# Scan matmuls of a hybrid HGRN2 and mLSTM block: full-array products in place of 64-row and 64-column ones

## The chip, the cores and the metric

One core of one Trainium2 chip runs one layer in one launch. The metric is device time in microseconds: the median of the runs of a kernel. All operands are float32.

## What is computed

One layer of a diffusion backbone for 128 prompt tokens and 256 sample tokens, width 2048: modulation (shift, scale and gate from silu(c) @ w_mod), a token mixer with an HGRN2 branch and an mLSTM branch, each scanned forward and backward with 8 heads, a merge, and a SwiGLU feed-forward net. The parts that the change touches, for one head and direction:

```
mod = silu(c) @ w_mod + b_mod                        # shift and scale of h
att = (q exp(b - b_ref)) (k exp(b_ref - b))^T        # HGRN2, causal, chunks of 64
qk  = (q k^T) exp(log_d - m_t)                       # mLSTM, m_t: row maximum
num = qk v + exp(g + m_0 - m_t) (q C_0)              # second term: the carried state
C   = sum_s exp(w_end - m) k_s v_s^T                 # new state of the prompt
```

mLSTM has 64 channels for q and k and 128 for v; HGRN2 has 128 for both.

## The kernel before

**The stream.** Every projection is W^T x with a 128x128 weight tile stationary and 384 tokens moving. Weights arrive in units of 1 MB (`load`, line 941, queue of SP), three on chip. Half a unit is a *piece*: 8 weight tiles. ScalarE rounds a piece to float32r (`wh`, line 356, called from `high`), VectorE makes the remainder (`wl`, line 953), and TensorE does three products a tile (lines 969 to 971), 24 a piece, 12,480 in all. Each accumulator is taken from PSUM by ScalarE or VectorE in `evac`.

**The work beside it.** The scans of both branches, the splits for the merge and the rest of the modulation are written as operations (`op(engine, cost, function, r=, w=)`), and `schedule` puts each in a slot before the products of a piece, in program order per engine, by its cost in us and its operands. `run_piece(i)` then issues: the load, `low(i + 1)`, the slot's operations, `high(i + 2)`, the products. So the costs written in the code set the order, not the time.

**Start.** For each of 16 column tiles j `mod1_half` makes rows of silu(c) @ w_mod in four column groups of the array, ScalarE copies them to `mvs`, and `mod1_end` (line 1099) sums the four groups: for shift and scale one product with `mvs` stationary and a 0/1 selector of two columns moving (line 1103). VectorE makes `shc` and `aac` of it (lines 1106, 1107), then `modulate` makes h's two parts.

**HGRN2, `hgrn(h)`.** GpSimd makes the cumulative sums (`cum`, lines 412 to 423). `fatt` (lines 479, 480) makes scores of 3 tiles of 128 tokens: the 128x128 product, then the block between the two chunks of the tile, 64x64, over part of it in PSUM. `fkt` transposes keys (line 487), `fds` makes state updates (line 498), `fo` the output (lines 517, 521).

**mLSTM rows, `rows()`.** The gates' cumulative sums run on GpSimd and the running maximum on VectorE, both through `scan` (lines 579 to 583), once per kernel, forward heads on partitions 0 to 7 and backward ones on 32 to 39. `fm` splits the row maxima M into `mh` and `ml`, 64 partitions each.

**mLSTM heads, `head(p, x, ...)`.** Two heads share a tile of q and of k, head x on partitions 64x to 64x + 63 (`rs`). `fqk` makes q k^T from 64 rows (lines 672 to 674). For each direction `fmb` spreads one row of M over 128 partitions with two products of 64 rows (lines 685, 686); VectorE adds the mask (`md`, line 690), ScalarE takes exponentials (`E`, `si`), VectorE multiplies (lines 708, 715, 716); `fnum` makes the numerator: intra products (line 727), and the carried term `si` times `c0`, 64 rows (line 730). `fcf` makes the new state, one product of 64 columns per direction (line 753); ScalarE copies it and GpSimd's queue writes it. Later the heads are normed and transposed (`fot`, line 786).

```
te.matmul(get(pa)[:, t], get(e2[d])[:, c], get(e1[d])[:, c], start=True, stop=True)
te.matmul(get(pa)[a0:a0 + 64, t, b0:b0 + 64], get(kl)[:, t], get(qb)[:, t], start=True, stop=True,
te.matmul(get(o)[:, l], get(si)[rs, (l - 1) * P:l * P], get(c0t)[rs, d], start=False, stop=True)
```

Of the kernel before, what the change touches and what calls it, by code (L numbers as in the profile page):

```python
# [37 lines left out]
# column starts in w_in  # L38
# [4 lines left out]
# columns of the packed vectors  # L43
# [8 lines left out]
V_SEL = 251  # L52
NVEC = 253

# columns of the constants
# [208 lines left out]
def body(ctx, tc, ws, wg, wm1, wm2, xt, vec, con, s0, c0, out_y, out_s, out_c, out_m, units, n_groups, late, trial):  # L264
    """late: the last piece beside which the scans run. trial: only plans, and returns where parts of it end."""
# [30 lines left out]
    # ================= the work beside the stream =================  # L296
    ops, tags, avail = [], {}, {}
    real, shapes = {}, {}
    for key, i in last_piece.items():
        if key[0] == "z":  # L300
            avail[key[1:]] = i
    Z = {}      # projected heads
    S = {}      # tiles that stay
    O = {}      # outputs of the heads

    caps = {"t": 7, "vn": 2, "s0": 2, "qb": 1, "kl": 1, "kp": 1, "kn": 1, "qx": 2, "dec": 2, "fin": 1, "s1": 2,
            "sc": 4, "o": 2, "c0": 2, "mkn": 2, "md": 1, "E": 2, "si": 2, "dn": 2, "hh": 2, "kw": 1, "cs": 1,
# [4 lines left out]
    for n in ("c0", "mkn", "md", "E", "si", "dn", "hh", "kw", "cs", "bst", "mv"):  # L312
        pool_of[n] = "mt"
# [52 lines left out]
    def hgrn(h):  # L366
# [34 lines left out]
        for d in range(2):  # L401
            w = lambda d=d: S["lw"][:, d, h:h + 1]  # noqa: E731
# [25 lines left out]
        for d in range(2):  # L428
            w = lambda d=d: S["lw"][:, d, h:h + 1]  # noqa: E731
# [46 lines left out]
            def fatt(d=d, pa=pa, kl=kl, qb=qb, a0=a0, b0=b0):  # L476
                for t in range(3):
                    c = slice(t * P, t * P + P)
                    te.matmul(get(pa)[:, t], get(e2[d])[:, c], get(e1[d])[:, c], start=True, stop=True)  # L479
                    te.matmul(get(pa)[a0:a0 + 64, t, b0:b0 + 64], get(kl)[:, t], get(qb)[:, t], start=True, stop=True,  # L480
                              skip_group_check=True)

            op("P", 1.0, fatt, r=[e1[d], e2[d], kl, qb], w=[pa])
# [62 lines left out]
    SEGS = ((0, NP), (NP, T))  # L546

    def rows():
# [46 lines left out]
        def fm():  # L595
# [3 lines left out]
            ve.tensor_copy(S["mh"], M)  # L599
            ve.tensor_tensor(S["ml"], M, S["mh"].bitcast(F32), ALU.subtract)  # L600
# [6 lines left out]
        op("D", 2.0, fm, r=["ra"], w=["rM", "rg", "we", "mh", "ml"])  # L607
# [43 lines left out]
    def head(p, x, mq, mk, c0t, kn, g):  # L651
# [26 lines left out]
        for d in range(2):  # L678
            i = 32 * d + h
            mb, md = N(f"mb{d}", "sc", (P, T)), N(f"md{d}", "md", (P, 3, P))  # L680
            e, si = N(f"e{d}", "E", (P, 4, P)), N(f"si{d}", "si", (P, 2 * P))

            def fmb(mb=mb, i=i):
                one = S["identr"][:, i:i + 1].to_broadcast([64, P])
                te.matmul(get(mb), one, S["mh"], start=True, stop=False)
                te.matmul(get(mb), one, S["ml"], start=False, stop=True)

            op("P", 0.33, fmb, r=["mh", "ml"], w=[mb], **g)
# [19 lines left out]
            op("D", cd(256), lambda si=si: ve.tensor_tensor(get(si)[rs], get(si)[rs], Z[mq][rs, NP:T], ALU.mult),  # L708
# [14 lines left out]
            def fnum(e=e, si=si, o=o, d=d, src=src):  # L723
                for l in range(3):
# [17 lines left out]
        kw, cf, cs = N("kw", "kw", (P, 2, 64)), N("cf", "sc", (64, 2, P + 1)), N("cs", "cs", (64, 2, P + 1))  # L742
# [141 lines left out]
    # ================= constants =================  # L884
# [10 lines left out]
    sel = vt[:, V_SEL:V_SEL + 2]  # L895
# [10 lines left out]
    # silu of the conditioning, padded to 32 columns  # L906
# [7 lines left out]
    # lower bound: softmax over the layer axis, first entry  # L914
# [19 lines left out]
    # ================= the weight stream =================  # L934
# [134 lines left out]
    # ================= start: modulation, h, the first heads =================  # L1069
# [14 lines left out]
    def mod1_half(j, half):  # L1084
        """Rows of silu(c) @ w_mod: four column tiles of the array at once, a quarter of k each."""
# [423 lines left out]
```

## Time and profile before

| | |
|---|---|
| median of 3 runs | 2459.87 us (2458.62 to 2460.76) |
| profiled execution, span from first to last instruction | 2456.4 us |
| TensorE busy | 2386.4 us, 14199 passes |
| VectorE, ScalarE, GpSimd busy | 1522.5, 929.1, 283.7 us |
| share of TensorE in the chain that ended last | 90% |

The profiled execution is known by its span alone; the runs' median is 3.4 us above it. In the profile a row of TensorE names the line, the tiles, then the array shape "rows\*columns", then the moving operand's partitions x elements. A float32 product is recorded as two passes, a float32r product or a transpose as one. Matmuls are pipelined: each lasts longer than the distance to the next, so distances between starts tell the rate. Times in rows are us from the span's start.

### The profile page before, as it was taken

To read this page: it belongs to the slowest core of one execution; us is meant where nothing else is said; L and a number is where in the kernel's file an instruction comes from. 1 tells how busy PE (TensorE), PEld (TensorE's weight loads), DVE (VectorE), ACT (ScalarE), POOL (GpSimd) and SP (SyncE) were. 2 spreads that over 40 slices of the span, in tenths; PEclk is the share of its full clock that TensorE was granted. 3 is DMA by queue.
4 is the path that set the end of the run, shared out by engine and by line. 5 is a ranking of instruction groups with operands and counts; after the bars stand their busy time and mean duration, and the time that the engine had idled before them with its cause. 6 is when DMAs were issued, how large, how long until landed. Compare 5 with 4: busy or idle time off the path is not lost.

```text
span 2456.4 us, 34520 instructions
## 1 busy us (share of the span) xinstructions
PE 2386.4 (97%) x14199; PEld 2313.9 (94%) x14199; DVE 1522.5 (62%) x2313; ACT 929.1 (38%) x1346; POOL 283.7 (12%) x332
## 2 busy tenths in 40 slices
PE   7999999999999999999996999999999999999995
PEld 5899889998999999999996999999999999999995
DVE  5777778776656888886758788334333433333337
ACT  5325555654445232223543333332233233223225
POOL 1115733320000000000415000000000000000002
PEclk9999999999999999999998999999999999999998
DMA  9863324333323666564432556333333333333331
GB/s 356 299 250 144 115 95 164 141 145 140 111 89 106 234 236 241 225 231 172 162 125 81 189 217 245 106 136 120 122 136 120 128 130 120 131 126 120 135 123 69
DMA packets 70541, 388.90 MB, mean 158 GB/s; under 512 B 8304, under 2 KB 10480, under 8 KB 37104
## 3 DMA queue, kind: packets, MB, share of 16 engines
q1 hardware_dynamic: 67824, 381.97, 42.3%
q0 software_dynamic: 1408, 3.16, 0.4%
q8 instruction: 111, 1.82, 0.3%
q10 hardware_dynamic: 1152, 1.57, 0.2%
q14 instruction: 46, 0.38, 0.0%
HBM read 381.95 MB, written 4.72 MB: 157 GB/s over the span
## 4 chain that ended last, share of the span: by engine, by line
PE 90%; DVE 5%; POOL 3%; ACT 1%; DMA 1%; issue 1%; SPq 0%; POOLq 0%; ACTq 0%; DVEq 0%
PE mm L969 28%; PE mm L971 28%; PE mm L970 28%; PE mv L1091 1%; DVE yacc L364 1%; PE o_o L727 1%; DVE wl L953 1%; POOL pp L579 1%; DVE modt L1059 1%; POOL cb L412 1%; PE o_o L730 1%; PE sc_pa L479 1%; DMA raw<-ws 1%; DVE lo L1064 0%; POOL pp L582 0%
## 5 line engine op out<-in xcount | busy, mean ns | idle before, releaser
L969 PE MATMUL mm<-hi,wh 128*128 128x384 f32 x3200 | 1088.9, 340 | 14.0 <-ACT hi L358 9.4
L971 PE MATMUL mm<-hi,wl 128*128 128x384 f32 x3200 | 1074.6, 336 | 8.4 <-DVE wl L953 8.4
L970 PE MATMUL mm<-lo,wh 128*128 128x384 f32 x3200 | 1073.7, 336 | 1.2 <-DVE lo L1064 1.2
L356 ACT ACTIVATE wh<-raw 128x1024 fp32r<-128x1024 f32 x520 | 548.5, 1055 | 557.2 <-PE mm L970 546.6
L953 DVE TENSOR_TENSOR wl<-raw,wh 128x1024 fp32r<-128x1024 f32 x520 | 635.9, 1234 | 64.7 <-ACT wh L356 64.4
L969 PEld LDWEIGHTS mm<-hi,wh 128*128 128x128 f32 x3200 | 604.2, 189 | 31.9 <-issue 14.0
L971 PEld LDWEIGHTS mm<-hi,wl 128*128 128x128 f32 x3200 | 603.8, 189 | 9.5 <-DVE wl L953 9.4
L970 PEld LDWEIGHTS mm<-lo,wh 128*128 128x128 f32 x3200 | 604.1, 189 | 3.2 <-DVE lo L1064 1.9
L815 DVE SCALAR_TENSOR_TENSOR acc_acc<-raw_w,st,acc_acc 128x512 f32<-128x512 f32 x480 | 335.1, 756 | 0.1
L969 PE MATMUL mm<-gh,wh 128*128 128x384 f32 x704 | 238.3, 338 | 0.0
L971 PE MATMUL mm<-gh,wl 128*128 128x384 f32 x704 | 238.0, 338 | 0.1
L970 PE MATMUL mm<-gl,wh 128*128 128x384 f32 x704 | 237.9, 338 | 0.0
L1048 DVE TENSOR_TENSOR yacc<-mm,yacc 128x384 f32<-128x384 f32 x80 | 44.6, 557 | 158.6 <-PE mm L971 158.6
L1033 DVE TENSOR_TENSOR fs<-mm,fs 128x384 f32<-128x384 f32 x44 | 24.6, 558 | 185.9 <-ACT fs L358 185.9
L364 POOL TENSOR_TENSOR yacc<-yacc,r 128x384 f32<-128x384 f32 (+1 forms) x6 | 7.5, 1247 | 1101.7 <-ACT r L358 1101.7
L971 PEld LDWEIGHTS mm<-gh,wl 128*128 128x128 f32 x704 | 132.2, 188 | 0.6 <-DVE wl L953 0.6
L969 PEld LDWEIGHTS mm<-gh,wh 128*128 128x128 f32 x704 | 132.2, 188 | 0.5 <-ACT yacc L356 0.4
L970 PEld LDWEIGHTS mm<-gl,wh 128*128 128x128 f32 x704 | 132.2, 188 | 0.4 <-DVE gl L844 0.4
L1038 DVE TENSOR_TENSOR fs<-mm,fs 128x384 f32<-128x384 f32 x44 | 24.5, 557 | 171.6 <-PE mm L971 171.6
L364 POOL TENSOR_TENSOR sum<-sum,part 128x384 f32<-128x384 f32 x29 | 34.5, 1189 | 510.5 <-ACT part L358 510.0
L970 PE MATMUL mm<-o,wh 128*128 128x384 f32 x256 | 86.3, 337 | 0.0
L969 PE MATMUL mm<-oh,wh 128*128 128x384 f32 x256 | 86.1, 337 | 0.0
(290 smaller groups left out, 1831.1 us busy)
## 6 DMA issues: line engine op xcount, KB each, us to landing
raw<-ws SPq DMA_DIRECT2D x260, 1024.0 KB, 4.9
raw_w<-wm SPq DMA_DIRECT2D x128, 512.0 KB, 3.4
wm<-wm SPq DMA_DIRECT2D x64, 512.0 KB, 6.4
xs<-xt SPq DMA_DIRECT2D x4, 768.0 KB, 7.0
x<-xt SPq DMA_DIRECT2D x4, 768.0 KB, 6.9
out_y<-yacc SPq DMA_DIRECT2D x8, 192.0 KB, 1.9
out_y<-yacc ACTq DMA_DIRECT2D x8, 192.0 KB, 1.9
s_s<-s POOLq DMA_DIRECT2D x8, 128.0 KB, 3.2
```

The source lines that it names most:

```text
L356: sc.activation(out, in_, func, bias=0.0, scale=scale)
L364: (gp if eng == "G" else ve).tensor_tensor(out, a, b, o)
L412: gp.tensor_tensor(y[:, :, 4:12], x[:, :, 4:12], x[:, :, 4 + sg * sh:12 + sg * sh], ALU.add)
L479: te.matmul(get(pa)[:, t], get(e2[d])[:, c], get(e1[d])[:, c], start=True, stop=True)
L579: en.tensor_tensor(Y[r, b + sh:e], X[r, b + sh:e], X[r, b:e - sh], o)
L815: ve.scalar_tensor_tensor(get(acc)[:, c], get(w)[:, i], col, get(acc)[:, c], ALU.mult, ALU.add)
L953: ve.tensor_tensor(lo, src, hi.bitcast(F32), ALU.subtract)
L969: te.matmul(acc, hi[:, s], xh, start=first, stop=False)
L970: te.matmul(acc, hi[:, s], xl, start=False, stop=False)
L971: te.matmul(acc, lo[:, s], xh, start=False, stop=last)
L1033: ve.tensor_tensor(s, acc, s, ALU.mult)
L1048: ve.tensor_tensor(yacc[j], acc, yacc[j], ALU.add)
```

## The change

- `fatt` issues its three 128x128 products first and its three 64x64 products after them; cost 1.0 to 0.8.
- `fm` writes M's two parts into one tile of 128 partitions, `mhl`; `identr` holds the identity twice, one below the other; `fmb` is one product of 128 rows; cost 0.33 to 0.17.
- `si` becomes four tiles that stay, 128 partitions high, whose half of the other head is set to zero once by GpSimd; `fnum` multiplies all 128 rows of `si` and `c0`; cost 1.3 to 1.2.
- `fcf` makes both directions in one product of 128 columns; the state's output has the order head, direction, key, value; cost 0.45 to 0.22, ScalarE's copy 258 to 129 columns.
- `mod1_end` transposes `mvs` (two transposes) and VectorE sums the four groups from PSUM (a reduction); the selector columns go; the constants, which hold the identity, are loaded before the first unit of the stream and not after it.
- Comments go, lines move by a few.

```diff
@@ plan of tiles
-            "sc": 4, "o": 2, "c0": 2, "mkn": 2, "md": 1, "E": 2, "si": 2, "dn": 2, "hh": 2, "kw": 1, "cs": 1,
+            "sc": 4, "o": 2, "c0": 2, "mkn": 2, "md": 1, "E": 2, "dn": 2, "hh": 2, "kw": 1, "cs": 1,
@@ fatt
                     te.matmul(get(pa)[:, t], get(e2[d])[:, c], get(e1[d])[:, c], start=True, stop=True)
+                for t in range(3):
                     te.matmul(get(pa)[a0:a0 + 64, t, b0:b0 + 64], get(kl)[:, t], get(qb)[:, t], start=True, stop=True,
                               skip_group_check=True)
-            op("P", 1.0, fatt, r=[e1[d], e2[d], kl, qb], w=[pa])
+            op("P", 0.8, fatt, r=[e1[d], e2[d], kl, qb], w=[pa])
@@ fm
-            ve.tensor_copy(S["mh"], M)
-            ve.tensor_tensor(S["ml"], M, S["mh"].bitcast(F32), ALU.subtract)
+            mh, ml = S["mhl"][0:64], S["mhl"][64:P]
+            ve.tensor_copy(mh, M)
+            ve.tensor_tensor(ml, M, mh.bitcast(F32), ALU.subtract)
@@ fmb
-                one = S["identr"][:, i:i + 1].to_broadcast([64, P])
-                te.matmul(get(mb), one, S["mh"], start=True, stop=False)
-                te.matmul(get(mb), one, S["ml"], start=False, stop=True)
-
-            op("P", 0.33, fmb, r=["mh", "ml"], w=[mb], **g)
+                te.matmul(get(mb), S["identr"][:, i:i + 1].to_broadcast([P, P]), S["mhl"], start=True, stop=True)
+
+            op("P", 0.17, fmb, r=["mhl"], w=[mb], **g)
@@ fnum
-                        te.matmul(get(o)[:, l], get(si)[rs, (l - 1) * P:l * P], get(c0t)[rs, d], start=False, stop=True)
+                        te.matmul(get(o)[:, l], S[si][:, (l - 1) * P:l * P], get(c0t)[:, d], start=False, stop=True)
-            op("P", 1.3, fnum, r=[e, si, va, c0t], w=[o], **g)
+            op("P", 1.2, fnum, r=[e, si, va, c0t], w=[o], **g)
@@ fcf
-            for d in range(2):
-                te.matmul(get(cf)[:, d], get(kw)[:, d], S[va][:, 0], start=True, stop=True)
-        op("P", 0.45, fcf, r=[kw, va], w=[cf], **g)
-        op("A", ca(258), lambda: act(get(cs), get(cf), AF.Copy), r=[cf], w=[cs], **g)
-        op("G", 1.1, lambda: gp.dma_start(out_c[h], get(cs)), r=[cs], **g)
+            te.matmul(get(cf), get(kw).rearrange("p d k -> p (d k)"), S[va][:, 0], start=True, stop=True)
+        op("P", 0.22, fcf, r=[kw, va], w=[cf], **g)
+        op("A", ca(P + 1), lambda: act(get(cs), get(cf), AF.Copy), r=[cf], w=[cs], **g)
+        op("G", 1.1, lambda: gp.dma_start(out_c[h].rearrange("d k v -> (d k) v"), get(cs)), r=[cs], **g)
@@ mod1_end
-        o = ps([P, 2, 2], "mvo", "sc", 3)
+        pt = ps([P, 2, P], "mvo", "sc", 3)
         for c in range(2):
-            te.matmul(o[:, c], sb[:, c * P:c * P + P], sel, start=True, stop=True)
+            te.transpose(pt[:, c], sb[:, c * P:c * P + P], S["ident"])
+        o = stp.tile([P, 2, 2], F32, tag="mvq", bufs=2, name="mvq")
+        ve.tensor_reduce(o, pt.rearrange("p s (q c) -> p s c q", c=32)[:, :, 0:2], mybir.AxisListType.X, ALU.add)
@@ start
     mod1_load(0)
+    sy.dma_start(ct, con)
     load(0)
-    sy.dma_start(ct, con)
@@ tiles
-    S["identr"] = mp.tile([64, 64], F32R, name="identr")
-    ve.tensor_copy(S["identr"], ct[0:64, 0:64])
+    S["identr"] = mp.tile([P, 64], F32R, name="identr")
+    for b in (0, 64):
+        ve.tensor_copy(S["identr"][b:b + 64], ct[b:b + 64, C_ID + b:C_ID + b + 64])
@@ mLSTM tiles
+        for d in range(2):
+            S[f"si{x}{d}"] = mtp.tile([P, 2 * P], F32, name=f"si{x}{d}")
+            gp.memset(S[f"si{x}{d}"][64 - 64 * x:P - 64 * x], 0.0)
```

How the order moves, in listings of the instructions as they are issued ("x2" is a row that repeats; sizes are those of the result, partitions x columns). First TensorE at the first `fatt` of the program, between the products of two pieces (sc_pa the scores, sc_pk the transposed keys). Before:

```order
L971 MATMUL mm<-hi,wl 128x384
L479 MATMUL sc_pa_2496<-t_e_2395,t_e_2389 128x128
L480 MATMUL sc_pa_2496<-qb_qb_2398,kl_kl_2444 64x64
L479 MATMUL sc_pa_2496<-t_e_2395,t_e_2389 128x128
L480 MATMUL sc_pa_2496<-qb_qb_2398,kl_kl_2444 64x64
L479 MATMUL sc_pa_2496<-t_e_2395,t_e_2389 128x128
L480 MATMUL sc_pa_2496<-qb_qb_2398,kl_kl_2444 64x64
L487 MATMUL sc_pk_2503<-ct,kp_kp_2446 128x128 x2
```

And with the change:

```order
L968 MATMUL mm<-hi,wl 128x384
L478 MATMUL sc_pa_2528<-t_e_2427,t_e_2421 128x128 x3
L480 MATMUL sc_pa_2528<-qb_qb_2430,kl_kl_2476 64x64 x3
L487 MATMUL sc_pk_2535<-ct,kp_kp_2478 128x128 x2
L966 MATMUL mm<-hi,wh 128x384
```

The six products are the same, in two runs of one shape.

Second, TensorE at the first numerators of mLSTM, at piece 100 (o_o the numerator, E_e the weights of the tokens, c_c the state c0, sc_pv the next head's values, sc_mb a row maximum). Before:

```order
L727 MATMUL o_o_5888<-va_5681,E_e_5788 128x129 x2
L730 MATMUL o_o_5888<-c_c_5688,si_si_5791 128x129
L727 MATMUL o_o_5888<-va_5681,E_e_5788 128x129 x2
L730 MATMUL o_o_5888<-c_c_5688,si_si_5791 128x129
L727 MATMUL o_o_5895<-va_5681,E_e_5796 128x129 x3
L730 MATMUL o_o_5895<-c_c_5688,si_si_5798 128x129
L727 MATMUL o_o_5895<-va_5681,E_e_5796 128x129
L730 MATMUL o_o_5895<-c_c_5688,si_si_5798 128x129
L664 MATMUL sc_pv<-ct,z_mv 128x128 x3
```

And with the change:

```order
L726 MATMUL o_o_5919<-va_5713,E_e_5827 128x129 x2
L729 MATMUL o_o_5919<-c_c_5728,si_5715 128x129
L726 MATMUL o_o_5919<-va_5713,E_e_5827 128x129 x2
L729 MATMUL o_o_5919<-c_c_5728,si_5715 128x129
L665 MATMUL sc_pv<-ct,z_mv 128x128 x3
L685 MATMUL sc_mb_5930<-mhl,identr 128x384
```

The backward numerator has moved to piece 101, and a row maximum of the next head, now one product, stands in its place.

Third, TensorE at the end of mLSTM with the change, pieces 126 and 127 (sc_ot the transposed output of the head before). Between the rows of line 685 and that of line 784 stand the 24 products of piece 126:

```order
L685 MATMUL sc_mb_7348<-mhl,identr 128x384
L685 MATMUL sc_mb_7356<-mhl,identr 128x384
...
L784 MATMUL sc_ot<-ct,hh_hh_7236 128x128 x3
L726 MATMUL o_o_7400<-va_5719,E_e_7352 128x129 x2
L729 MATMUL o_o_7400<-c_c_6630,si_5721 128x129
```

The numerator of the last head stands one piece behind its row maximum; before, no numerator stood closer than two pieces. The same distance of one piece stands at pieces 124 and 125.

## Rows read from the trace of the kernel before

**Rows 1.** The page's first line.
```profile
span 2456.4 us, 34520 instructions
```
**Rows 2.** Table by stretches: busy us (instructions) of each engine, granted clock, DMA share, GB/s.
```profile
208.00:292.00 84.00, 78.83 (x474) 75.66 (x474) 62.97 (x102) 48.09 (x78) 70.34 (x105) 1.00 0.37 143
326.00:762.00 436.00, 434.10 (x2570) 405.18 (x2570) 293.77 (x553) 224.49 (x400) 76.64 (x100) 1.00 0.34 123
292.50:295.90 3.40, 3.40 (x13) 3.40 (x12) 3.30 (x10) 3.37 (x7) 1.64 (x3) 0.50 0.21 58
```
**Rows 3.** TensorE's timeline: start, duration, instruction; the stream's products.
```profile
394.74 0.33 PE L969 MATMUL mm<-hi,wh 128*128 128x384 f32 x1
...
400.80 0.34 PE L971 MATMUL mm<-hi,wl 128*128 128x384 f32 x1
```
**Rows 4.** The same timeline: an output of HGRN2, all on the full array.
```profile
344.30 0.60 PE L517 MATMUL o_po<-t_as,vn_vn 128*128 128x128 f32 x4
...
346.03 0.34 PE L970 MATMUL mm<-lo,wh 128*128 128x384 f32 x1
```
**Rows 5.** The same timeline: one cycle of `fatt` and the start of the next.
```profile
410.93 0.49 PE L479 MATMUL sc_pa<-t_e,t_e 128*128 128x128 f32 x2 [1.32 <-DVE t_e L446]
411.34 0.33 PE L480 MATMUL sc_pa<-qb_qb,kl_kl 128*64 128x64 f32 x2
411.60 0.49 PE L479 MATMUL sc_pa<-t_e,t_e 128*128 128x128 f32 x2
```
**Rows 6.** The same timeline: transposes of 64 columns in the row work.
```profile
316.79 0.22 PE L621 MATMUL sc_rt<-ct,rg 64*128 64x64 f32 x1
...
317.10 0.22 PE L622 MATMUL sc_rt<-ct,we 64*128 64x64 f32 x1
```
**Rows 7.** Timeline of GpSimd, VectorE, TensorE near 290 us, idle time before and its releaser.
```profile
285.09 1.00 POOL L364 TENSOR_TENSOR ra<-ra,rg 64x384 f32<-64x384 f32 x1
286.13 1.49 DVE L579 TENSOR_TENSOR pp<-ra 32x127 f32<-32x127 f32 x1 [5.70 <-POOL ra L364]
291.40 0.49 PE L521 MATMUL o_po<-qx_qx,s_s 128*128 128x128 f32 x2 [3.54 <-DVE s_s L505]
```
**Rows 8.** TensorE's timeline: first pass of one head's numerators, and what follows them.
```profile
572.06 0.61 PE L727 MATMUL o_o<-va,E_e 128*128 128x129 f32 x4
...
576.19 0.55 PE L664 MATMUL sc_pv<-ct,z_mv 128*128 128x128 f32 x3
```
**Rows 9.** The same timeline: a row maximum beside q k of the other rows.
```profile
581.18 0.38 PE L673 MATMUL sc_qa<-z_mq,z_mk 64*128 64x256 f32 x1
581.18 0.44 PE L685 MATMUL sc_mb<-mh,identr 64*128 64x384 f32 x1
```
**Rows 10.** The same timeline: the products around a row maximum that stands alone.
```profile
557.10 0.34 PE L971 MATMUL mm<-hi,wl 128*128 128x384 f32 x1
...
558.19 0.34 PE L970 MATMUL mm<-lo,wh 128*128 128x384 f32 x1
```
**Rows 11.** The same timeline: the products around a new state that stands alone.
```profile
566.92 0.34 PE L971 MATMUL mm<-hi,wl 128*128 128x384 f32 x1
...
568.05 0.33 PE L970 MATMUL mm<-lo,wh 128*128 128x384 f32 x1
```
**Rows 12.** Timeline of TensorE and VectorE at `mod1_end` of j = 2.
```profile
44.42 0.50 PE L1103 MATMUL mvo<-vt,mvs 128*128 128x2 f32 x4
...
45.04 0.33 PE L970 MATMUL mm<-lo,wh 128*128 128x384 f32 x1
45.09 0.21 DVE L1106 TENSOR_SCALAR shc<-mvo,vt 128x2 f32<-128x2 f32 x1
```
**Rows 13.** Timeline: a row maximum and the last VectorE operation on its E.
```profile
721.10 0.42 PE L685 MATMUL sc_mb<-mh,identr 64*128 64x384 f32 x1
...
725.76 0.41 DVE L716 TENSOR_TENSOR E_e<-E_e,sc_qb 128x256 f32<-128x256 f32 x1
```
**Rows 14.** DMA issues of the first 60 us: KB each, median us to landing.
```profile
raw<-ws SPq DMA_DIRECT2D x5, 1024.0 KB, 12.4
```

More of the change, by code (lines that the diff above doesn't have):

```diff
@@ L51 @@
 V_C = 219
-V_SEL = 251
-NVEC = 253
+NVEC = 251
 C_ID, C_UP, C_LO, C_BUP, C_BLO = 0, 128, 256, 384, 512
@@ L311, in body @@
         pool_of[n] = "hg"
-    for n in ("c0", "mkn", "md", "E", "si", "dn", "hh", "kw", "cs", "bst", "mv"):
+    for n in ("c0", "mkn", "md", "E", "dn", "hh", "kw", "cs", "bst", "mv"):
         pool_of[n] = "mt"
@@ L605, in fm @@
             ve.tensor_scalar(we, a[:, 0:NP], S["mT"], None, ALU.subtract)
-        op("D", 2.0, fm, r=["ra"], w=["rM", "rg", "we", "mh", "ml"])
+        op("D", 2.0, fm, r=["ra"], w=["rM", "rg", "we", "mhl"])
         def fmo():
@@ L680, in head @@
             mb, md = N(f"mb{d}", "sc", (P, T)), N(f"md{d}", "md", (P, 3, P))
-            e, si = N(f"e{d}", "E", (P, 4, P)), N(f"si{d}", "si", (P, 2 * P))
+            e, si = N(f"e{d}", "E", (P, 4, P)), f"si{x}{d}"
             def fmb(mb=mb, i=i):
-                one = S["identr"][:, i:i + 1].to_broadcast([64, P])
-                te.matmul(get(mb), one, S["mh"], start=True, stop=False)
-                te.matmul(get(mb), one, S["ml"], start=False, stop=True)
-            op("P", 0.33, fmb, r=["mh", "ml"], w=[mb], **g)
+                te.matmul(get(mb), S["identr"][:, i:i + 1].to_broadcast([P, P]), S["mhl"], start=True, stop=True)
+            op("P", 0.17, fmb, r=["mhl"], w=[mb], **g)
             c = C_BLO if d else C_BUP
@@ L698, in foff @@
                 cc = V_M0B + 8 * d + h
-                act(get(si)[rs], get(mb)[rs, NP:T], AF.Exp, bias=S["vt"][rs, cc:cc + 1], scale=-1.0)
+                act(S[si][rs], get(mb)[rs, NP:T], AF.Exp, bias=S["vt"][rs, cc:cc + 1], scale=-1.0)
             op("A", ca(P) + ca(256), foff, r=[mb, "ac"], w=[e, si], table="E", **g)
@@ L707, in head @@
             op("A", 3 * ca(P), fdiag, r=[md, "ac"], w=[e], table="E", **g)
-            op("D", cd(256), lambda si=si: ve.tensor_tensor(get(si)[rs], get(si)[rs], Z[mq][rs, NP:T], ALU.mult),
+            op("D", cd(256), lambda si=si: ve.tensor_tensor(S[si][rs], S[si][rs], Z[mq][rs, NP:T], ALU.mult),
                r=[mq], w=[si], **g)
@@ L741, in head @@
             op("D", cd(T) + 0.2, fh, r=[o, dn, "ac"], w=[hh[d], dn], **g)
-        kw, cf, cs = N("kw", "kw", (P, 2, 64)), N("cf", "sc", (64, 2, P + 1)), N("cs", "cs", (64, 2, P + 1))
+        kw, cf, cs = N("kw", "kw", (P, 2, 64)), N("cf", "sc", (P, P + 1)), N("cs", "cs", (P, P + 1))
         def fkw():
@@ L894, in body @@
     S["ident"] = ct[:, C_ID:C_ID + P]
-    sel = vt[:, V_SEL:V_SEL + 2]
     for n, v in (("eps", EPS), ("one", 1.0), ("zero", 0.0)):
@@ L1180, in body @@
     mp = open_pool("mk")
-    S["identr"] = mp.tile([64, 64], F32R, name="identr")
-    ve.tensor_copy(S["identr"], ct[0:64, 0:64])
-    S["mh"] = mp.tile([64, T], F32R, name="mh")
-    S["ml"] = mp.tile([64, T], F32R, name="ml")
+    S["identr"] = mp.tile([P, 64], F32R, name="identr")
+    for b in (0, 64):
+        ve.tensor_copy(S["identr"][b:b + 64], ct[b:b + 64, C_ID + b:C_ID + b + 64])
+    S["mhl"] = mp.tile([P, T], F32R, name="mhl")
     S["ac"] = mp.tile([P, 3, 64], F32, name="ac")
@@ L1456, in layout @@
     c0 = np.ascontiguousarray(cn.reshape(2, 4, P, P + 1).transpose(1, 2, 0, 3))
-    for q in range(4):
-        for k in range(2):
-            v[32 * q + k, V_SEL + k] = 1
     return {"ws": ws, "wg": wg, "wm1": wm1, "wm2": wm2, "xt": xt, "vec": v, "con": constants(), "s0": s0, "c0": c0}
-OUTS = {"out_y": (P, KT, T), "out_s": (2, 8, P, P), "out_c": (8, 64, 2, P + 1), "out_m": (2, 8, 1)}
+OUTS = {"out_y": (P, KT, T), "out_s": (2, 8, P, P), "out_c": (8, 2, 64, P + 1), "out_m": (2, 8, 1)}
 def find_lead():
@@ L1503 @@
     s, cn, m = (np.asarray(got[k]) for k in ("out_s", "out_c", "out_m"))
-    c = cn[..., 0:P].transpose(2, 0, 1, 3)
-    n = cn[..., P].transpose(2, 0, 1)
+    c = cn[..., 0:P].transpose(1, 0, 2, 3)
+    n = cn[..., P].transpose(1, 0, 2)
     r = np.ascontiguousarray
```

## The prediction

> **What bounds the kernel now.** I read the page first: the span is 2456.4 us [rows 1]. The median of the runs, 2459.87 us, is 3.4 us above it; I take that 3.4 us as what lies around the span and work against the span. Then I read the table by stretches: from 326 to 762 us, where most of the edited work lies, TensorE is busy 434 of 436 us at full clock, VectorE 294, ScalarE 224, GpSimd 77 [rows 2]. So there a nanosecond of TensorE is a nanosecond of the kernel. From 208 to 292 us it is another picture: GpSimd is busy 70 of 84 us and TensorE has waits [rows 2].
>
> Since matmuls overlap, busy time tells little; I read the timeline of TensorE and take distances between starts. The stream's products start 6.06 us apart over 35 steps, 0.173 us each [rows 3]; a piece of 24 of them is 4.16 us. For the other work I take the distance from the last start before it, less what the products alone would need. A float32 product is two passes in the records ("x2" is one product), a transpose one. In the plain case, seven products of 128 columns on the full array (14 passes, lines 517 and 521 in turn, other operands each time) take 1.73 us to the second product after them; less one step of 0.173 that is **0.111 us a pass**, say 0.112 [rows 4].
>
> Against this price, a pass that follows one of another array shape (the "128\*128", "128\*64", "64\*128" of a row) is dear. In `fatt` the same pair of lines returns every 0.67 us [rows 5]: two passes of 128 columns (0.224) and two of 64. Seven small transposes of 64 columns show 0.31 us for five steps, 0.062 a pass [rows 6]. So 0.67 - 0.224 - 0.124 = **0.32 us is two changes of shape**.
>
> **The change part by part.**
>
> *`fatt`* (16 times: 8 heads, 2 directions). Three shape cycles become one. Two cycles at 0.67 turn into four passes of each kind, 4 x 0.112 + 4 x 0.062 = 0.70: it saves 1.34 - 0.70 = 0.64 us each time. If a 64-column pass without a change cost 0.13 (half of the 0.26 us from 411.34 to 411.60 [rows 5], which holds a change), it would be 1.34 - 0.97 = 0.37. I take 0.64, since the small pass has a row of its own. But four of the 16 lie in the stretch from 208 to 292 us, where the pace is not TensorE's. At 291.40 TensorE has stood 3.54 us for VectorE's s_s (line 505), which stands in VectorE's queue behind the row scans of line 579, which at 286.13 had waited for GpSimd's ra [rows 7]. GpSimd is the bound of that stretch, so these four only lengthen the wait: 12 x 0.64 = **7.7 us** (4.4 to 7.7; 10.3 if all sixteen counted).
>
> *`fnum`, the carried term* (16 times). Both directions of one head, 24 passes, take from 572.06 to 576.19, 4.13 us [rows 8]. The zero-padded si lets all 24 run on the full array: 24 x 0.112 = 2.69, so 1.44 a head, 11.5 for eight. What is lost: a 64-row pass can run beside one that uses the other 64 rows. In two heads, and no more, the last c0 product of before runs beside the next head's line 672, in the way that lines 673 and 685 start together at 581.18 [rows 9]. A c0 product with its two changes costs (4.13 - 16 x 0.112) / 4 = 0.58, so at most 2 x 0.58 = 1.2 goes: **10.3 us**. The memsets of si on GpSimd are free: it is busy 77 of 436 us there [rows 2]; uncovered they would delay only the load of c0, which is issued several pieces before its first use.
>
> *`fmb`, row maxima* (16 times). Two 64-row products become one of 128 rows, one step of 0.173. Alone, the two cost 558.19 - 557.10 - 2 x 0.173 = 0.74 [rows 10]. Six stand alone; six stand in company and share a change of shape, which I count at 0.35 to 0.74; four stand beside the q k products of the other 64 rows and cost nothing [rows 9]. So 12 x 0.65 = 7.8 goes, 16 x 0.173 = 2.8 comes, **5.0 us**.
>
> *`fcf`* (8 times). Four passes become two. Alone: 568.05 - 566.92 - 2 x 0.173 = 0.78 [rows 11], new 0.224, so 0.56. Five of the eight follow a pass that had another shape anyway and pay one change less; mean 0.45: **3.6 us**. The copy and the write of the state get no longer and nobody waits for them.
>
> *`mod1_end`* (16 times). Four passes take (45.04 - 44.42 - 0.173) / 4 = 0.112 each although they move two columns [rows 12]; two transposes take two such passes, which saves 0.22. VectorE gets one reduction more before shc. Its price has no row: at least 0.21 (shc, which reads PSUM [rows 12]), at most 0.41 (a 128x256 operation from PSUM, line 716 [rows 13]); with 16 numbers read I take 0.21. It hides except for the first three j, where VectorE still adds partial sums and TensorE waits for it; there the saving is lost and the reduction paid. 13 x 0.22 - 3 x 0.21 = **2.3 us** (1.6 to 2.9).
>
> The constants (320 KB) now load ahead of the first unit. In the crowded start a unit of 1024 KB lands 12.4 us after its issue [rows 14]; 320 KB in front of it cost at most that share, 3.9 us, and at least nothing. I take nothing: ScalarE comes to the first unit only after the first hi, which hangs on x, the shift and the scale; that chain is the cover.
>
> *New waits.* TensorE's order stays the same up to piece 79 of the stream; in the mLSTM part the planner packs the shorter TensorE work tighter. From a row-max product to the end of its E (line 716) the chain takes 721.10 to 726.17, 5.07 us [rows 13]; in two places (the last listing in front shows one) the numerator now stands one piece behind the row-max product, 4.16 + 0.2. That is 0.7 us twice; with 0.6, a guess, for the tighter rest I take **-2 us** (0 to -8 if chains wait in every head).
>
> Sum: 7.7 + 10.3 + 5.0 + 3.6 + 2.3 - 2 = **26.9 us**. The span becomes 2429.5 and the time **2433.0 us**.
>
> A rule speaks against this change. The Trainium skill, "TensorEngine Tiling (Array Packing)", section Overview, has operands of at most 64 rows run as independent tiles, up to twice as fast. Were every c0 pass of before shared in that way, giving it up would cost another 32 x 0.112 = 3.6 us, and the sum would be 23.3 us, 2436.6; the trace shows such pairs in six places only [rows 9], since elsewhere the neighbour uses all rows.
>
> **Rivals.**
> 1. *Waits take half of the mLSTM gain.* The shorter slots leave VectorE and ScalarE less cover, and each of eight heads has two chains of about 5 us. One more microsecond in ten of the sixteen: 2433 + 10 = 2443. For it: one-piece distances are new. Against it: VectorE is busy 294 of 436 us, and almost nothing waits there now [rows 2].
> 2. *More comes through.* No new waits, and the absorbed four count: 2433 - 2 - 2.6 = 2428; without the lost overlap 2427.
> 3. *The cost is not the shape.* If only removed passes count, fmb wins (24 - 16) x 0.173 = 1.4, fcf 8 x 0.224 = 1.8, mod1_end 2.3, and 1.2 of overlap and 2 of waits are lost: 2.3 us, 2457.6, no change. Against it: lines 517 and 521 change operands without any extra [rows 4].
> 4. *Slower, by the clock.* After the 3.54 us wait the granted clock is 0.50 from 292.5 to 295.9, the lower of its two levels [rows 2, 7]. If the waits for E grow so long that TensorE's clock falls each time, one occurrence costs its wait and 4.16 us more for a piece at half clock. With 0.7 us waits it decides from 28.9 / 4.9, six occurrences; eight, one a head, are 39 us against 28.9 won, 2470. Against it: from 208 to 292 us TensorE's waits are 84.0 - 78.8 = 5.2 us in all and the clock is 1.00 [rows 2]; only after the longest of them did it fall, so 0.7 us should do nothing.
>
> **How the numbers follow.** The forecast, 2428 to 2440, has 0.70. Rival 1 (2440 to 2450) has 0.17, rival 2 below 2428 0.07, rival 3 0.04, rival 4 0.02. A range of 2426 to 2446 takes in rival 2 and the greater part of rival 1 and leaves out less than 0.2. A measurement of this kernel can tell about 0.2%, 4.9 us: faster 0.94, same 0.04, slower 0.02.
>
> **What would show it.** Right: `fatt` at about 1.35 us from its first pass to the transposes behind it, against three cycles of 0.67 now; a head's numerators at 2.7 us; row-max products 0.17 apart from their neighbours; no 64\*128 passes except q k and the seven small transposes; the wait for s_s near 290 us longer by 2 to 3 us; GpSimd's chain from 208 to 292 as long as now. Wrong: passes still 0.2 apart in runs of one shape (rival 3); waits of TensorE for E, hh or si between 550 and 762 us of over 5 us in all (rival 1); stretches of clock 0.5 there (rival 4).

## The result and the profile after

The changed kernel takes 2431.9 us (median of 4 runs, 2431.28 to 2432.88) beside 2459.24 us for the kernel before on the same chip: a ratio of 0.9887, 95% interval 0.9873 to 0.9901. The forecast was 2433.0 us. A second set of its runs gave 2429.64 us (2428.59 to 2433.35), ratio 0.9881 (0.9866 to 0.9895). One execution of one kernel below, 8628 us for e8_fatt_cut, is left out of all figures: its other three lie between 2438.8 and 2439.2, and no profile explains it.

The page's first line, then the table by stretches of the changed kernel (columns as in [rows 2]):

```profile
span 2429.2 us, 34432 instructions
```
```profile
208.00:292.00 84.00, 77.79 (x471) 75.61 (x470) 63.93 (x104) 47.57 (x77) 70.83 (x105) 0.98 0.38 145
326.00:762.00 436.00, 432.74 (x2689) 421.68 (x2688) 316.59 (x585) 240.29 (x427) 76.04 (x104) 1.00 0.37 136
49.90:53.30 3.40, 3.40 (x26) 2.05 (x28) 2.33 (x6) 0.00 (x0) 0.00 (x0) 0.50 0.02 5
271.70:275.10 3.40, 3.40 (x13) 3.40 (x12) 3.00 (x6) 2.29 (x5) 3.24 (x7) 0.50 0.00 0
```

The span is 27.2 us shorter. From 326 to 762 us TensorE is as full as it was [rows 2], but 2689 passes fit where 2570 did: the window holds more of the program. The stretch from 208 to 292 us did not get emptier on GpSimd (70.83 us against 70.34). Two stretches at the lower clock level, at 50 and 272 us, are new, and one that the trace of before has at 326.6 to 330.0 us is gone.

Now the edited places, in TensorE's timeline (start, duration, instruction). One `fatt` that nothing waits for:

```profile
437.81 0.34 PE L968 MATMUL mm<-hi,wl 128*128 128x384 f32 x1
437.99 0.83 PE L478 MATMUL sc_pa<-t_e,t_e 128*128 128x128 f32 x6
438.75 0.56 PE L480 MATMUL sc_pa<-qb_qb,kl_kl 128*64 128x64 f32 x6
439.24 0.44 PE L487 MATMUL sc_pk<-ct,kp_kp 128*128 128x128 f32 x2
439.44 0.42 PE L966 MATMUL mm<-hi,wh 128*128 128x384 f32 x1
```

From its first pass to the transposes (line 487): 439.24 - 437.99 = 1.25 us; to the product behind them 1.45. The same block in the trace of before, three cycles as in [rows 5], takes 446.03 - 443.91 = 2.12:

```profile
443.91 0.38 PE L479 MATMUL sc_pa<-t_e,t_e 128*128 128x128 f32 x2
...
446.03 0.42 PE L969 MATMUL mm<-hi,wh 128*128 128x384 f32 x1
```

One head's numerators, against 4.13 us [rows 8]:

```profile
579.21 0.61 PE L726 MATMUL o_o<-va,E_e 128*128 128x129 f32 x4
579.66 0.39 PE L729 MATMUL o_o<-c_c,si 128*128 128x129 f32 x2
...
581.81 0.42 PE L966 MATMUL mm<-hi,wh 128*128 128x384 f32 x1
```

24 passes in 2.60 us, 0.108 each; line 729, the carried term, now stands in the middle of line 726 without a seam. A row maximum alone (before: [rows 10]) and a new state alone (before: [rows 11]):

```profile
547.88 0.34 PE L968 MATMUL mm<-hi,wl 128*128 128x384 f32 x1
548.05 0.34 PE L685 MATMUL sc_mb<-mhl,identr 128*128 128x384 f32 x1
548.23 0.34 PE L966 MATMUL mm<-hi,wh 128*128 128x384 f32 x1
...
556.61 0.34 PE L968 MATMUL mm<-hi,wl 128*128 128x384 f32 x1
556.78 0.38 PE L751 MATMUL sc_cf<-va,kw_kw 128*128 128x129 f32 x2
556.92 0.42 PE L966 MATMUL mm<-hi,wh 128*128 128x384 f32 x1
557.18 0.33 PE L967 MATMUL mm<-lo,wh 128*128 128x384 f32 x1
```

The row maximum is one step among the stream's, 0.18 us where 0.74 went; the state costs 557.18 - 556.61 - 2 x 0.173 = 0.22 where 0.78 went. `mod1_end` at j = 2, TensorE and VectorE (before: [rows 12]):

```profile
44.23 0.38 PE L1100 MATMUL mvo<-ct,mvs 128*128 128x128 f32 x2
...
44.62 0.33 PE L967 MATMUL mm<-lo,wh 128*128 128x384 f32 x1
44.91 0.17 DVE L1102 TENSOR_REDUCE mvq<-mvo 128x4 f32<-128x16 f32 x1
45.10 0.23 DVE L1105 TENSOR_SCALAR shc<-mvq,vt 128x2 f32<-128x2 f32 x1
```

Two passes at 0.11 in place of four, and a reduction of 0.17 us before shc. Last, four waits of TensorE in the changed kernel (idle time and its releaser in brackets):

```profile
270.36 0.71 PE L498 MATMUL sc_pd<-vn_vn,kn_kn 128*128 128x128 f32 x4 [2.06 <-ACT kn_kn L355]
290.91 0.49 PE L521 MATMUL o_po<-qx_qx,s_s 128*128 128x128 f32 x2 [3.10 <-DVE s_s L505]
500.77 0.44 PE L487 MATMUL sc_pk<-ct,kp_kp 128*128 128x128 f32 x2 [0.50 <-DVE kp_kp L468]
713.83 0.71 PE L726 MATMUL o_o<-va,E_e 128*128 128x129 f32 x4 [0.67 <-DVE E_e L714]
```

The first is about twice as long as before (1.14 us), the second shorter than the 3.54 of [rows 7], the last two are new.

**Where the time went, by stage.** The stream is the same 12,480 products in every kernel here, so it is a ruler. I take the starts of its products number 120, 773, 1183, 2304 and 3161 (59.8, 204.9, 299.8, 551.0 and 765.0 us in the trace of before), counted from the first product, and subtract before. Negative is faster, in us. After the last mark no kernel differs by more than 0.25. The labels are those of the experiments below.

| kernel | to 60 | 60-205 | 205-300 | 300-551 | 551-765 |
|---|---|---|---|---|---|
| changed | +1.73 | -2.48 | +0.45 | -8.72 | -18.21 |
| changed, again (e11_again) | -1.35 | -2.48 | +0.50 | -7.10 | -18.22 |
| e1_fatt | -1.17 | 0.00 | -0.14 | -7.92 | 0.00 |
| e2_fnum | -0.33 | 0.00 | -0.01 | -0.02 | -9.87 |
| e3_fmb | -1.24 | 0.00 | -0.12 | +3.10 | -4.91 |
| e4_fcf | -0.30 | 0.00 | +0.04 | +0.02 | -3.33 |
| e5_mod | -0.52 | -2.48 | +1.20 | +1.44 | 0.00 |
| e6_oldcosts | +1.47 | -2.48 | +0.07 | -6.89 | -19.53 |
| e7_before_cut | -0.78 | 0.00 | -7.34 | -0.15 | 0.00 |
| e8_fatt_cut | -1.28 | 0.00 | -10.03 | -8.09 | 0.00 |
| e9_sel3 | -1.38 | -2.48 | +1.26 | -7.29 | -18.22 |
| e10_pad | -1.14 | -2.48 | -1.51 | -4.76 | -22.70 |
| e12_scan | -0.99 | -2.48 | -3.45 | -14.61 | -20.64 |

The columns 60-205 and 551-765 repeat to 0.01 us where the code is the same. The others carry stretches of low clock that come and go (last section), some 1.6 us each; "to 60" spreads by 1.3 us even among the kernels whose code is that of before there.

### The profile page after: what moved, and what is told of

It reads as the page before. It is cut to its first block, busy times and chain, and to the rows that moved or that the text cites. A ratio compares the mean times of both kernels' runs of the same rounds, so it can differ in the third digit from the quotient of the medians.

```text
span 2429.2 us, 34432 instructions
## 1 busy us (share of the span) xinstructions
PE 2355.8 (97%) x14135; PEld 2300.5 (95%) x14135; DVE 1527.1 (63%) x2330; ACT 928.2 (38%) x1346; POOL 283.8 (12%) x336
## 4 chain that ended last, share of the span: by engine, by line
PE 88%; DVE 6%; POOL 3%; ACT 2%; issue 1%; POOLq 0%; ACTq 0%; DVEq 0%
PE mm L966 28%; PE mm L968 27%; PE mm L967 27%; PE mv L1088 1%; DVE wl L950 1%; DVE yacc L363 1%; POOL cb L411 1%; POOL pp L579 1%; PE o_o L726 1%; DVE modt L1056 1%; DVE lo L1061 0%; PE sc_pa L821 0%; POOL pp L582 0%; ACT sq L357 0%; POOL sb L420 0%
## 5 line engine op out<-in xcount | busy, mean ns | idle before, releaser
L363 POOL TENSOR_TENSOR sum<-sum,part 128x384 f32<-128x384 f32 x29 | 34.3, 1183 | 499.6 <-ACT part L357 499.1
L355 ACT ACTIVATE gh<-fs 128x384 fp32r<-128x384 f32 x44 | 23.0, 524 | 166.4 <-DVE fs L1035 166.4
```

The lines of the kernel that those rows point to most:

```text
L355: sc.activation(out, in_, func, bias=0.0, scale=scale)
L363: (gp if eng == "G" else ve).tensor_tensor(out, a, b, o)
```

## The experiments

My theory (S in the expectations) was that TensorE pays for each change of array shape, that the five gains add, and that GpSimd's chain before 300 us swallows four of the sixteen in `fatt`. The rivals: only passes that go away count (P); the new order of the planner makes or breaks the gain; something other than GpSimd swallows.

**Each part alone, on the kernel before, with the planner's costs left alone so that the order stays.**

```diff
 e1_fatt
                     te.matmul(get(pa)[:, t], get(e2[d])[:, c], get(e1[d])[:, c], start=True, stop=True)
+                for t in range(3):
                     te.matmul(get(pa)[a0:a0 + 64, t, b0:b0 + 64], get(kl)[:, t], get(qb)[:, t], start=True, stop=True,
 e2_fnum
-                        te.matmul(get(o)[:, l], get(si)[rs, (l - 1) * P:l * P], get(c0t)[rs, d], start=False, stop=True)
+                        te.matmul(get(o)[:, l], S[si][:, (l - 1) * P:l * P], get(c0t)[:, d], start=False, stop=True)
 e3_fmb
-                te.matmul(get(mb), one, S["mh"], start=True, stop=False)
-                te.matmul(get(mb), one, S["ml"], start=False, stop=True)
+                te.matmul(get(mb), S["identr"][:, i:i + 1].to_broadcast([P, P]), S["mhl"], start=True, stop=True)
 e4_fcf
-            for d in range(2):
-                te.matmul(get(cf)[:, d], get(kw)[:, d], S[va][:, 0], start=True, stop=True)
+            te.matmul(get(cf), get(kw).rearrange("p d k -> p (d k)"), S[va][:, 0], start=True, stop=True)
```

> The kernel before with fatt's two loops alone, its cost left at 1.0, so that nothing else moves. Theory S (the change of array shape costs, and the stretch from 208 to 292 us, paced by GpSimd, swallows four of the sixteen): 12 x 0.67 = 8.0 us faster, some 2451 us; up to 324 us in the trace only 0.5 us won, the rest between 324 and 550. Theory A (no absorption): 16 x 0.67 = 10.7, 2448.5. Theory P (only passes that are removed count): no change, 2459.

> The kernel before with the zero-padded si alone, cost left at 1.3. Theory S: 8 heads x 1.5 us less 1.2 for two lost pairs of c0 beside q k: 10.3 to 11 us faster, some 2448.5 us, a head's numerators 2.67 us. Theory P: as many passes as before and lost pairs, 1 us slower, 2460. Rival W (the shorter slots turn into waits for E): under 6 us faster, and waits before line 727 or its kin over 4 us in all.

> The kernel before with one 128-row row-maximum product alone, cost left at 0.33. Theory S: 5.0 us faster (six alone at 0.56, six in company at about 0.3, four beside q k nothing or slightly slower), 2454. Theory P: 1.4 us faster, 2458.

> The kernel before with both directions' new state in one product of 128 columns alone, costs left. Theory S: 3.6 us faster (0.56 where it stands alone, 0.4 elsewhere), 2455.6. Theory P: 8 x 0.224 = 1.8 us, 2457.4. Both are near what the measurement can tell, so the distances between products in the trace decide: 0.22 a state where it was 0.78.

Measured, beside 2459.89 us for the kernel before (21 runs): 2449.98 us (ratio 0.9963, 0.995 to 0.9975), 2450.14 (0.9962, 0.9949 to 0.9974), 2454.75 (0.998, 0.9971 to 0.9989) and 2455.6 (0.9985, 0.9977 to 0.9994). (The zeroed tiles, the stacked tile and the order of the state's output, which these edits need, are as in the change.) In the stages that hold the edits: -8.06, -9.87, -4.91 and -3.33 us. Theory P falls with the first: it removes no pass at all, keeps the rest of the order, and wins 8 us. The second also keeps its passes and wins 9.9, a little under the 10.3 to 11 expected, with 575.12 - 572.45 = 2.67 us for a head's numerators:

```profile
572.45 0.61 PE L727 MATMUL o_o<-va,E_e 128*128 128x129 f32 x4
...
575.12 0.49 PE L664 MATMUL sc_pv<-ct,z_mv 128*128 128x128 f32 x3
```

In the last the trace decides: a state alone costs 0.23 us.

One more rival has to be met. e1_fatt also moves each 64x64 product away from the 128x128 product whose block of PSUM it writes over, so it could have won by that and not by the shape. e2_fnum rules this out as the general cause: it leaves the order and the place in PSUM as they were, its carried term adds to the block that the pass before has just written, and at full shape that goes at 0.11 us a pass. The changes of shape, counted in the traces, give the same price from three edits: 28 fewer and 4.69 us in e1_fatt (products 1715 to 2304), 54 fewer and 9.87 us in e2_fnum, 16 fewer and 3.17 us in e10_pad (below, beside e6_oldcosts), that is 0.17 to 0.20 us a change.

Where did the four `fatt` before 300 us go? TensorE's waits in e1_fatt from 204 to 299 us (waiting tile <- engine and tile waited for: us in total, times, longest):

```profile
PE o_po L522 <- DVE s_s L506: 4.4, 2, 4.2
PE sc_pd L499 <- ACT kn_kn L356: 2.0, 1, 2.0
PE sc_pa L481 <- DVE kl_kl L466: 0.3, 1, 0.3
PE sc_ss L527 <- ACT t_sq L358: 0.3, 1, 0.3
PE sc_pk L488 <- DVE kp_kp L469: 0.2, 1, 0.2
```

And in the kernel before, from 205 to 300 us:

```profile
PE o_po L521 <- DVE s_s L505: 3.5, 1, 3.5
PE sc_pd L498 <- ACT kn_kn L356: 1.1, 1, 1.1
PE sc_pa L480 <- DVE kl_kl L466: 0.5, 1, 0.5
```

7.2 us in all, where before had 5.2: of the 2.7 us won there 2.1 came back as waiting, spread over most of them. Stage 205-300 gained 0.14; the 0.5 between has no wait in the trace.

**`mod1_end` alone, and the order alone.** e5_mod is the kernel before with the transposes, the reduction and the constants' earlier load; e6_oldcosts is the changed kernel with the costs of before, all five of them:

```diff
-            op("P", 0.8, fatt, r=[e1[d], e2[d], kl, qb], w=[pa])
+            op("P", 1.0, fatt, r=[e1[d], e2[d], kl, qb], w=[pa])
...
-            op("P", 1.2, fnum, r=[e, si, va, c0t], w=[o], **g)
+            op("P", 1.3, fnum, r=[e, si, va, c0t], w=[o], **g)
```

> The kernel before with mod1_end's transposes and reduction, and the constants loaded ahead of the first unit, and nothing else. As predicted: 13 x 0.22 - 3 x 0.21 = 2.3 us faster, 2457. Theory W (read from the trace of the whole change): the reduction lengthens the chain to hi in the first places, TensorE stands 0.4 us longer there twice, and a stretch of half clock follows at about 50 us that costs some 0.8 us: 0.5 to 1.0 us won at 200 us in the trace, 2458.5. If the constants' earlier load held up the first unit, the first product of the stream would start later than the 30 us of before.

> The kernel with the whole change, but the planner's costs as before (1.0, 0.33, 1.3, 0.45 for TensorE, 258 columns for ScalarE's copy), so that the order is that of before wherever tiles allow. Theory S (the products' shape makes the gain): within 2 us of the whole change, 2431 to 2434. Rival O (the order matters): 5 us or more away from 2431.9, slower if the tighter packing is part of the gain, faster if the one-piece distances cost.

e5_mod: 2457.82 us beside 2460.38 (ratio 0.9993, 0.9984 to 1.0002), by itself not to be told from no change; but between 60 and 205 us it wins 2.48, the same as every kernel with this edit. With the first 60 us (0.52, which is within the spread of that column) it is 3.0 ahead at 205 us, not 0.5 to 1.0: there is no low clock at 50 us in it, though TensorE's waits there are those of the changed kernel (0.77 and 1.80 us). Theory W was wrong about the price. e6_oldcosts: 2429.55 us (0.9876, 0.9862 to 0.9889); by the runs it cannot be told from the changed kernel. By the stages the new order costs 1.3 us from 551 to 765, where the wait for E at 713.83 is absent from e6_oldcosts, and in 420 to 551 us 0.7 us (-3.99 against -4.69, marks at products 1715 and 2304), where the wait for kp at 500.77 is absent. The theory holds: 2.0 us are the order's. The two waits make 1.2 of them; the other 0.8 has no wait in the trace and is open.

**Who swallows the four.** In both kernels the gate sums on GpSimd are cut to one step a segment; the other steps are left out, so the mLSTM gates are not those of the layer:

```diff
-                        def one(x=x, y=y, r=r, b=b, e=e, sh=sh, d=d):
+                        def one(x=src if o == ALU.add else x, y=y, r=r, b=b, e=e, sh=sh, d=d):
+                            if o == ALU.add and y != dst:
+                                return
```

> The kernel before with the sums of the gate scan on GpSimd cut to one step a segment: the other steps are left out, so the mLSTM gates are not what the layer asks for, and GpSimd has some 30 of its 70 us less between 208 and 292 us. It is the base for the next kernel. If GpSimd paces that stretch, TensorE's waits there (5.2 us, of which 3.5 for s_s) mostly go and the stream is 3 to 5 us ahead of the kernel before at 300 us. If VectorE's row maxima pace it, or the clock, less than 1 us.

> The same with fatt's two loops as well (the same gate sums are left out). Theory S with absorption by GpSimd: without GpSimd's chain all sixteen count, 16 x 0.67 = 10.7 us below the kernel with the cut scan alone, and of it 2.7 between 205 and 300 us, where the kernel with fatt alone won 0.1. Rival B (something other than GpSimd swallows the four): 8 us again, under 0.7 of it before 300 us.

2449.88 us and 2439.02 us, 10.9 apart. The stretch from 208 to 292 us in the one and the other:

```profile
208.00:292.00 84.00, 84.00 (x507) 81.18 (x506) 70.13 (x137) 55.87 (x90) 44.91 (x55) 1.00 0.41 156
```
```profile
208.00:292.00 84.00, 83.99 (x519) 82.36 (x517) 72.73 (x146) 56.41 (x90) 44.95 (x55) 1.00 0.40 152
```

The cut alone wins 7.3 us in that stage, more than expected: the 5.2 us of waits, and the low clock behind the longest of them [rows 2]. With GpSimd at 45 us instead of 70, TensorE does not wait once in the stage from 205 to 300, and `fatt`'s gain there is 10.03 - 7.34 = 2.69 us, 4 x 0.67, where it was 0.14. Over the whole of `fatt` it is 10.64, 16 x 0.67. Rival B falls.

**The first places of `mod1_end`.**

```diff
+        if j < 3:
+            o = pt[:, :, 0:2]
+            for c in range(2):
+                te.matmul(o[:, c], sb[:, c * P:c * P + P], sel, start=True, stop=True)
```

> The whole change, but with the old product by the selector for the first three j of mod1_end, where TensorE waits for what comes after it. Theory R (the reduction in VectorE's chain makes those waits longer and brings on the stretch of half clock at 50 us): waits at 35 and 47 us back to 0.4 and 1.37 us, no half clock at 50, 1.5 to 2.5 us faster than the whole change, 2429.5 to 2430.5. Theory C (the clock falls there by its own rule, whatever the wait): 0.6 us faster from the shorter waits less 0.67 for three savings given up, that is the same as the whole change within 0.5, 2431.5 to 2432.

> The changed kernel once more, beside the others on one chip: 2431 to 2433 us. If the stretches of half clock come and go from one execution to the next, its times fall in groups 1.5 to 2.5 us apart, and its profile shows other stretches than the first; if they belong to the program, the same ones at 50, 272 and 292 us.

e9_sel3: 2430.6 us (ratio 0.9881, 0.9864 to 0.9897). Its waits in the start, and behind them the low-clock table of e11_again:

```profile
21.71 0.69 PE L968 MATMUL mm<-hi,wh 128*128 128x384 f32 x1 [2.82 <-ACT wh L356]
35.23 0.44 PE L968 MATMUL mm<-hi,wh 128*128 128x384 f32 x1 [0.44 <-ACT z_g L356]
47.73 0.44 PE L968 MATMUL mm<-hi,wh 128*128 128x384 f32 x1 [1.33 <-DVE z_g L1011]
```
```profile
49.90:53.30 3.40, 2.83 (x54) 1.42 (x45) 1.76 (x7) 0.39 (x1) 0.00 (x0) 1.00 0.61 189
323.10:326.50 3.40, 3.40 (x13) 3.40 (x12) 3.14 (x11) 3.05 (x5) 0.00 (x0) 0.50 0.85 301
```

In the changed kernel the three waits are 3.05, 0.76 and 1.79 us, together 1.0 longer, so the reduction does lengthen them. But theory R's other half falls: the same program a second time runs at full clock at 50 us, and at half clock at 323 instead. No time was won that the runs or the stages show: to 60 us, -1.38 against -1.35 for e11_again, and its median lies between the two of the changed kernel.

**A version beyond both.** In e10_pad `fqk` is made full as well; in e12_scan the row scans also run over all three blocks of 128 tokens at once, with the total of one block added to the next at the end.

```diff
+        op("A", ca(T), lambda: act(S[kz][rs], Z[mk][rs], AF.Copy), r=[mk], w=[kz], **g)
...
-            te.matmul(get(qa)[:, 0:NP], k[rs, 0:NP], q[rs, 0:NP], start=True, stop=True)
+            te.matmul(get(qa)[:, 0:NP], k[:, 0:NP], q[:, 0:NP], start=True, stop=True)
```
```diff
-                                en.tensor_tensor(Y[r, b + sh:e], X[r, b + sh:e], X[r, b:e - sh], o)
+                            en.tensor_tensor(Y[:, :, sh:P], X[:, :, sh:P], X[:, :, 0:P - sh], o)
```

> The whole change with the planner's costs as before, and q k made full too: ScalarE copies the head's 64 rows of k into a tile whose other half is zero, and line 673 and its kin multiply 128 rows; one buffer of c0 in place of two makes the room. Theory S: q k of a head from 1.48 us extra to 1.07 (128 + 256 + 256 columns at full-array rates), 8 x 0.4 = 3.2 us faster than without it, 2426.5. Theory P (passes and columns as before): the same as without it, 2429.5, or 3 us slower by the eight copies on ScalarE and the lost buffer.

> The kernel with the padded k (costs as before), and the row scans rewritten so that nothing is left out: all three blocks of 128 tokens in one instruction a step and one addition of a block's total at the end, 15 instructions a direction where there were 30. From the rows of GpSimd between 208 and 292 us (sums 26, copies 14 us in that stretch) some 15 us of its work there go, half of what the cut scan took away. Theory S with GpSimd as the bound before 300 us: half to all of the 7 us that the cut scan won, 3 to 8 us below the 2426.8 us of the kernel with padded k. If one of the other engines paces the stretch once GpSimd has 15 us less: under 2 us.

e10_pad: 2426.77 us (ratio 0.9866, 0.9851 to 0.988). Its q k in TensorE's timeline, on the full array, right behind a carried term:

```profile
563.00 0.39 PE L675 MATMUL sc_qa<-z_mq,kz 128*128 128x128 f32 x2
563.23 0.60 PE L676 MATMUL sc_qa<-z_mq,kz 128*128 128x256 f32 x2
563.66 0.59 PE L677 MATMUL sc_qb<-z_mq,kz 128*128 128x256 f32 x2
563.90 0.52 PE L968 MATMUL mm<-hi,wh 128*128 128x384 f32 x1
564.26 0.33 PE L969 MATMUL mm<-lo,wh 128*128 128x384 f32 x1
```

564.26 - 563.00 - 0.173 = 1.09 us. From 551 to 765 us it is 22.70 - 19.53 = 3.17 us ahead of e6_oldcosts, 8 x 0.40, as expected.

e12_scan: 2416.95 us (ratio 0.983, 0.9817 to 0.9844), the fastest kernel here, 42.8 us below the one before (2459.77 beside it). It is 9.8 us below e10_pad, more than the 3 to 8 us expected, and mostly not where it was expected. From 208 to 292 us:

```profile
208.00:292.00 84.00, 77.94 (x483) 76.36 (x483) 74.78 (x116) 51.43 (x83) 65.14 (x77) 1.00 0.39 143
```

GpSimd is down by 7 us only (72.12 in e10_pad), since the instructions are fewer but longer. VectorE is now at 75, and TensorE still waits 6.0 us between 205 and 300 (5.8 in e10_pad), 5.1 of it for VectorE. So before 300 us the expectation's other branch holds: another engine sets the pace. The 1.9 us won there are about the price of one low-clock stretch, which e10_pad has at 269.0 to 272.4 us and e12_scan has not.

The greater part came later. From 205 to 765 us TensorE's waits are 13.5 us in e10_pad and 8.9 in e12_scan, mostly because two waits for t_e are gone, one of 1.3 us near 406 us and this one:

```profile
322.27 1.01 PE L478 MATMUL sc_pa<-t_e,t_e 128*128 128x128 f32 x3 [5.21 <-DVE t_e L445]
```

It is no matter of GpSimd's gate sums alone: in e7_before_cut, where they are cut, TensorE still waits 3.0 us there (3.2 in before). e12_scan also shortens VectorE's row maxima and moves the order; which of the two removes the waits was not separated. And no stretch of low clock lies between 28 and 1260 us, where the trace of e10_pad has 10.2 us of them, at 1.6 us for 3.4 an estimated 4.8. With the 4.6 us of waits that is a little more than the 8.6 us between the two traces.

## Why the prediction was right, and where it was not

| term | predicted | shown | by |
|---|---|---|---|
| `fatt`, 12 of 16 | 7.7 | 8.1 | e1_fatt, 205 to 551 |
| `fnum` | 10.3 | 9.9 | e2_fnum, 551 to 765 |
| `fmb` | 5.0 | 4.9 | e3_fmb |
| `fcf` | 3.6 | 3.3 | e4_fcf |
| `mod1_end` | 2.3 | 2.3 | 2.48 + 0.21 - (1.0 - 3 x 0.21), in part an estimate |
| order and new waits | -2 | -2.0 | changed against e6_oldcosts |
| parts together in mLSTM | 0 | +1.4 | 19.53 - (9.87 + 4.91 + 3.33) |
| sum | 26.9 | 27.9 | spans differ by 27.2 and 28.6 |

- **The price of the shape.** `fatt` loses four changes and 0.67 us, 0.17 a change; the prediction read 0.32 for two out of [rows 5, 6]. The Trainium skill, "TensorEngine Tiling (Array Packing)", section Tiling Modes, says that changing the tiling mode drains TensorE; the trace fits that: it shows a cost of 0.17 us a change here, though not by what mechanism. The Overview of the same page of the Trainium skill, weighed in the prediction, would have made the gain of `fnum` some 3.6 us smaller; e2_fnum shows 9.9 of the 10.3 predicted, so the sharing of 64-row passes was as rare as [rows 9] had it.
- **Absorption.** The step "GpSimd is the bound of that stretch" was right and is now shown by e7_before_cut and e8_fatt_cut. Its consequence was misread: the wait for s_s was to grow by 2 to 3 us. It grew by 0.7 in e1_fatt and fell to 3.10 in the changed kernel. 2.1 of the 2.7 us came back in e1_fatt, most of it at other waits; in the changed kernel the waits of that stage are only 1.0 us longer, and the low clock from 271.7 to 275.1, at some 1.6 us a stretch, takes more than the rest. The chain that sets the pace of a stretch hands TensorE several operands, and it can wait at each of them.
- **`mod1_end`.** The reduction takes 0.17 us for the 0.21 assumed. The 12 places after 60 us gave 2.48 us, 0.21 each, as reckoned; the fourth, before the mark, is put at the same. At the first three the prediction counted the saving as lost and the reduction as paid, which is waits longer by 0.43 each; they grew by 1.0 us in all, 0.34 each, so the net loss there is some 0.4 us and not 0.63.
- **New waits.** The -2 us was partly a guess and the mechanism was half right: waits for E and kp with the new order make up about 1.2 us of the 2.0. E waited once, not twice. That the sum fits so closely is luck. That the three mLSTM parts are worth 1.4 us more together than singly was not foreseen: beside each other, one part alone can only move a change of shape from one product to its neighbour. The traces have 109 changes from 551 to 765 us before, 54, 19 and 11 fewer with one part and 91 fewer with all; the 7 more, at 0.17 to 0.20, are 1.2 to 1.4 us.
- **Rivals.** 1 would have needed over 5 us of waits between 550 and 762; there are 1.3, and 0.6 of them, for z_mv, were there before. Of 2, the absorbed four count only once GpSimd is relieved. 3 fell with e1_fatt. 4 did not occur: no low clock lies between 296 and 1275 us in the changed kernel's trace. Its price was wrong too: 4.16 us is a whole piece at half clock, but the stretch in [rows 2] lasts 3.4 us, and one such stretch costs some 1.6.

## What to carry to other kernels

Read the array shape in the rows and count its changes, not only the columns: a short product of another shape in a stream of full ones can cost more in changes than in columns, and regrouping, stacking or zero-padding it to the full array paid here even with more multiplications by zero. Ask in each stretch who sets the pace before a gain is counted: the same 0.67 us were worth all or almost nothing, and relieving GpSimd of most of its gate sums gave back the four that were lost. A smaller relief did not (e12_scan): TensorE then waited for VectorE as long as before. Where the same stream of products runs in every variant, the start of the n-th product compares kernels by stage far more sharply than the total.

## What the runs showed of the hardware that was not expected

The half-clock stretches move between executions of one program: between the first 30 us and 1270 us, the changed kernel had them at 50, 272 and 292 us in one trace, at 268, 289 and 323 us in the other. From 300 to 345 us, where the one has none and the other 3.4 us, they differ by 1.6 us. With them the totals of one kernel spread by up to 5 us (2428.59 to 2433.35). A wait does not decide it alone: after a wait of 2.06 us for kn the clock is 0.50 from 271.7 us in the changed kernel, after one of 2.03 us in e1_fatt it is not. A wait of 1.3 us for t_e between 397 and 412 us stands in every trace but that of e12_scan; half clock follows it in two, e3_fmb (412.6 us) and e5_mod (410.3 us). What else decides is open.
